# A third pair of k-tiles with seven block products in each gate and up chunk, and in the last down pass

## The chip, the cores and the metric

The kernel runs on one core of a Trainium2 chip. The metric is the device time in microseconds (us) of one execution; the median of several runs is what is compared. TensorE (PE in the views) multiplies, VectorE (DVE) and ScalarE (ACT) work element by element, SyncE (SP) issues the DMAs, GpSimd (POOL) is nearly idle here.

## The reference, cut to what matters

One transformer-like layer on 256 rows of 2048 channels, in float32: a SwiGLU feed-forward, a mixer (sparse attention beside a spatial gate), and a second SwiGLU feed-forward. The change touches the two feed-forwards only.

```python
D_MODEL, SEQ, D_FF = 2048, 256, 5632

def swiglu(h, w_gate, w_up, w_down):
    return (jax.nn.silu(h @ w_gate) * (h @ w_up)) @ w_down

x = x + 0.5 * swiglu(rms_norm(x, norm_ffn1), ffn1_w_gate, ffn1_w_up, ffn1_w_down)
...
x = x + 0.5 * swiglu(rms_norm(x, norm_ffn2), ffn2_w_gate, ffn2_w_up, ffn2_w_down)
```

## The kernel before

Every float32 product is made of three matmuls: weights and activations are each split into a high part that TensorE takes whole and a low rest (`split_to`, lines 228 and 229: a copy on ScalarE gives `wh`, a subtraction on VectorE gives `wl`), and high by high, low by high and high by low are added in PSUM. The three matmuls of a product are lines 322 to 324 in `gemm_seven` and 280 to 282 in the plain `gemm`; each has 512 columns.

A feed-forward (`ffn`) walks over 11 chunks of 512 hidden channels. A chunk multiplies the 256 rows by 512 gate columns and 512 up columns over 16 k-tiles of 128. The first chunk or chunks (two in the first feed-forward, one in the second, `plain`) use the plain `gemm`; in the second plain chunk of the first feed-forward the activations are rescaled as well (`rescale`), and the sums of activation blocks are made there (`x_sums`). The other 19 chunks of the two feed-forwards use `gemm_seven`. After 6 chunks, and again after the last 5, the hidden activations are multiplied by the down weights in two passes of 1024 output columns each (`half` 0 and 1), again with `gemm_seven`, over 12 and then 10 pairs of k-tiles.

`gemm_seven` takes the k-tiles in pairs. A pair with two tiles of rows and two blocks of 512 columns is a 2 by 2 by 2 product of blocks. An ordinary pair makes eight block products (24 matmuls) from two split tiles of 1024 columns. A pair in `seven` makes seven (21 matmuls), with Winograd's sums: four sums of weight blocks, which VectorE forms in lines 336, 337, 338 and 345, and four sums of activation blocks, formed once by `block_sums` (lines 500 to 503). Such a pair splits two tiles of 1024 columns of `w`, one of 1024 columns of `T` and one of 512 columns of `T`. The results P1, P5, P6 and P7 stay in banks of their own; once the last seven-product pair is done they are added to `e` (or to `xres`) by the stages of `early` (lines 603 to 613 for a chunk), one stage at each `tick()`, and ordinary pairs alone tick. P2 and P3 sit in the two `tr` banks, so matmuls into them show as `tr<-`.

At the end of a chunk VectorE reads P2, P3, P4 and C22 with lines 621 and 624, ScalarE makes the silu (line 622), VectorE the product (line 625). In the ticks of the next chunk the result is turned: ScalarE makes planes (line 377), a DMA transpose from SP's queue (line 379) turns them, ScalarE joins them (line 381), then they are split, and for up to four chunks of a part `sum_chunk` makes the activation sums of the down pass.

Raw weights have three buffers `w` of two k-tiles (1 MB each, loaded by two DMAs of 512 KB from SP's queue, line 566, or one of 1 MB, line 370); the split tiles have four buffers `wh` and four `wl`, `T` has two. The order of instructions on each engine is made by a scheduler ahead of time, so that it differs from the order in the source; each engine then works through its own list strictly in that order.

Of the kernel before, what the change touches and what calls it, by code (L numbers as in the profile page):

```python
# [13 lines left out]
F32 = mybir.dt.float32  # L14
# [7 lines left out]
P = 128  # L22
# [44 lines left out]
def block_kernel(ctx: ExitStack, tc: tile.TileContext, x, positions, norm_ffn1, ffn1_w_gate, ffn1_w_up,  # L67
                 ffn1_w_down, norm_mix, w_in, q_norm, k_norm, idx_k_norm, sgu_v_norm, sgu_w_s, sgu_b_s,
                 w_up_attn, w_up_sgu, w_out, norm_ffn2, ffn2_w_gate, ffn2_w_up, ffn2_w_down, out):
    nc = tc.nc  # L70
# [12 lines left out]
    def uid(s):  # L83
        cnt[0] += 1
        return f"{s}_{cnt[0]}"
# [7 lines left out]
    def bank(shape=None):  # L93
        return psA.tile(shape or [P, 512], F32, tag="acc", name=uid("acc"))

    def trbank(shape):
        return psT.tile(shape, F32, tag="tr", name=uid("tr"))
# [7 lines left out]
    def tick(n=1):  # L105
        for _ in range(min(n, len(pending))):
            pending.popleft()()
# [119 lines left out]
    def split_to(hi, lo, src):  # L227
        nc.scalar.copy(hi, src)  # L228
        nc.vector.tensor_sub(lo, src, hi.bitcast(F32))  # L229
# [59 lines left out]
    def split_wide(src):  # L289
        n = src.shape[-1]  # L290
        whi = wsp.tile([P, 1024], F32R, tag="wh", name=uid("wh"))
        wlo = wsp.tile([P, 1024], F32R, tag="wl", name=uid("wl"))
        split_to(whi[:, :n], wlo[:, :n], src)
        return [(whi[:, o:o + 512], wlo[:, o:o + 512]) for o in range(0, n, 512)]

    def gemm_seven(new_T, xs, sums, nk, load, seven, early):

        acc = {}
        total = {}
        np_ = nk // 2
        for name in ("P1", "P5", "P6", "P7"):
            total[name] = len(seven)
        for name in ("P2", "P3", "P4"):  # L310
            total[name] = len(seven) + 2 * (np_ - len(seven))
        total["C22"] = 2 * (np_ - len(seven))
        done = {k: 0 for k in total}

        def product(name, st, w):
            (sh, sl), (wh, wl) = st, w
            if name not in acc:
                acc[name] = trbank([P, 512]) if name in ("P2", "P3") else bank()
            first = done[name] == 0
            done[name] += 1  # L320
            last = done[name] == total[name]
            nc.tensor.matmul(acc[name], sh, wh, start=first, stop=False)  # L322
            nc.tensor.matmul(acc[name], sl, wh, start=False, stop=False)  # L323
            nc.tensor.matmul(acc[name], sh, wl, start=False, stop=last)  # L324

        left = len(seven)
        wait = None
        for g in range(np_):
            w = wraw.tile([P, 2048], F32, tag="w", name=uid("w"))
            load(2 * g, 2, w.rearrange("p (k c) -> p k c", k=2))  # L330
            if g in seven:
                A11, A12, A22 = xs(2 * g, 0), xs(2 * g + 1, 0), xs(2 * g + 1, 1)
                S1, S2, S3, S4 = sums(g)
                T = new_T()
                B11, B12, B21, B22 = (w[:, i * 512:(i + 1) * 512] for i in range(4))
                nc.vector.tensor_sub(T[:, 0:512], B12, B11)
                nc.vector.tensor_sub(B12, B22, B12)
                nc.vector.tensor_add(T[:, 512:1024], B12, B11)
                b11, t3 = split_wide(w[:, 0:1024])
                product("P1", A11, b11)  # L340
                product("P7", S3, t3)
                t1, t2 = split_wide(T[:, 0:1024])
                product("P5", S1, t1)
                product("P6", S2, t2)
                nc.vector.tensor_sub(T[:, 1024:1536], B21, T[:, 512:1024])
                b21, b22 = split_wide(w[:, 1024:2048])
                product("P2", A12, b21)
                product("P3", S4, b22)
                t4, = split_wide(T[:, 1024:1536])
                product("P4", A22, t4)  # L350
                left -= 1
                if left == 0:
                    wait = 2
            else:
                for kk in range(2):
                    k = 2 * g + kk
                    B = split_wide(w[:, kk * 1024:(kk + 1) * 1024])
                    for t, names in enumerate((("P2", "P3"), ("P4", "C22"))):
                        for j, name in enumerate(names):
                            product(name, xs(k, t), B[j])  # L360
                    if wait is not None:
                        wait -= 1
                        if wait == 0:
                            pending.extendleft(reversed(early(acc["P1"], acc["P5"], acc["P6"], acc["P7"])))
                    tick()
        return [[acc["P2"], acc["P3"]], [acc["P4"], acc["C22"]]]
# [136 lines left out]
        nc.vector.tensor_sub(s_[:, 3, :], A12, s_[:, 1, :])  # L503
        split_to(hi, lo, s_)

    XSEVEN = (0, 3)
    PARTS = ((0, 6, (4, 4)), (6, 5, (4, 2)))
    KP = 24

    def ffn(nrm, wg, wu, wd, after_chunk, first=0, lead=None, plain=1):  # L510
        with tc.tile_pool(name=uid("ffn"), bufs=1) as pool:
            def new_T():
                return pool.tile([P, 3 * 512], F32, tag="T", bufs=2, name=uid("T"))


            xSh = pool.tile([P, len(XSEVEN), 4, P], F32R, name=uid("xSh"))
            xSl = pool.tile([P, len(XSEVEN), 4, P], F32R, name=uid("xSl"))

            def x_sums(i, f=None):
                k = 2 * XSEVEN[i]  # L520
                if f is None:
                    f = ttile([P, 2, S])
                    nc.vector.tensor_add(f, nrm.h[:, k:k + 2, :].bitcast(F32), nrm.l[:, k:k + 2, :].bitcast(F32))
                block_sums(xSh[:, i], xSl[:, i], f[:, 0, 0:P], f[:, 1, 0:P], f[:, 0, P:S], f[:, 1, P:S])
# [4 lines left out]
            def xsums(g):  # L529
                i = XSEVEN.index(g)  # L530
                return [(xSh[:, i, c, :], xSl[:, i, c, :]) for c in range(4)]

            def rescale(kp):
                f = nrm.apply(kp)
                if kp in XSEVEN:
                    x_sums(XSEVEN.index(kp), f)

# [3 lines left out]

            for f0, nf, nseven in PARTS:
                last_part = f0 + nf == FF // 512
# [17 lines left out]
                for fi in range(nf):  # L561
# [32 lines left out]
                    else:  # L594
# [3 lines left out]
                        def early(P1, P5, P6, P7, e=e):  # L598
# [17 lines left out]
                            return [one, two, three, four]  # L616

                        b = gemm_seven(new_T, xx, xsums, KD, load, XSEVEN, early)
                        for t in range(NT):
                            sg = ttile()  # L620
# [15 lines left out]
                for half in range(2):  # L636
                    c0 = half * 1024

                    def early(P1, P5, P6, P7, c0=c0):
# [23 lines left out]
                        def five():  # L663
                            nc.vector.tensor_add(right, right, q["5"][:, None, :].to_broadcast([P, 2, 512]))

                        return [one, two, three, four, five]

                    b = gemm_seven(new_T, xs, sums, nf * 4, loader(wd[f0 * 512:(f0 + nf) * 512, :], c0, 1024),
                                   [2 * i for i in range(nseven[half])], early)
                    for t in range(NT):  # L670
# [396 lines left out]
```

## Time and profile before

| | |
|---|---|
| Median of 3 runs | 2054.71 us (2052.78 to 2056.4) |
| The profiled execution's own time | 2055.26 us |
| Its span, first to last instruction | 2053.5 us |
| PE busy | 2039.0 us (99%), 9124 matmuls |
| Weight loads (PEld) busy | 1695.1 us (83%) |
| DVE busy | 1574.2 us (77%) |
| ACT busy | 1230.7 us (60%) |

The own time is 1.8 us longer than the span: what lies before the first and after the last instruction. Busy time is the union of an engine's instructions; an average over the span mixes stages, so the stages are looked at one by one below.

### The profile page before, as it was taken

Reading aid. Unit: us, or ns where it says so; the run is one execution under the profiler, and the core shown is the slowest. Engines: PE = TensorE matmul, PEld = TensorE weight load, DVE = VectorE, ACT = ScalarE, POOL = GpSimd, SP = SyncE. Lnnn points to the kernel's source line nnn. Section 1 sums busy time; section 2 is a strip of 40 time slices with the busy share of each in tenths; the row PEclk is TensorE's granted clock in tenths of the full one; section 3 lists DMA queues with packets and bytes.
Section 4 is the critical chain, followed back from the end, with each engine's and each line's share of the span. In section 5 each row is a group of like instructions: output and inputs, shape, how many; then the busy total and the mean of one; then the engine's idle time right before and its main releaser. Section 6 shows DMA issues by size and latency. Waiting matters only on the chain.

```text
span 2053.5 us, 25205 instructions
## 1 busy us (share of the span) xinstructions
PE 2039.0 (99%) x9124; PEld 1695.1 (83%) x9124; DVE 1574.2 (77%) x2043; ACT 1230.7 (60%) x1482; POOL 33.8 (2%) x62
## 2 busy tenths in 40 slices
PE   8999999999999999999999999999999999999999
PEld 7888888888888898888888888888888888888887
DVE  6888888788889667877544467568888888788895
ACT  6666664465666566656544445576666644666663
POOL 1000000000000000110000000000000000000000
PEclk9999999999999999999999999999999999999999
DMA  7666665667666676586655567776677666676674
GB/s 257 187 213 211 226 202 204 205 201 229 195 200 220 201 243 210 178 232 186 205 193 201 186 195 229 215 220 195 202 219 222 196 212 206 200 224 207 195 232 148
DMA packets 251533, 426.13 MB, mean 208 GB/s; under 512 B 106664, under 2 KB 108768, under 8 KB 251408
## 3 DMA queue, kind: packets, MB, share of 16 engines
q1 hardware_dynamic: 250880, 423.29, 65.3%
q0 software_dynamic: 528, 1.23, 0.4%
q8 instruction: 71, 1.16, 0.2%
q14 instruction: 54, 0.44, 0.1%
HBM read 398.26 MB, written 2.10 MB: 195 GB/s over the span
## 4 chain that ended last, share of the span: by engine, by line
PE 51%; DMA 1%; ACT 1%; DVE 0%; issue 0%; SPq 0%; DVEq 0%; ACTq 0%
PE acc L282 7%; PE acc L281 7%; PE acc L280 7%; PE acc L324 6%; PE acc L322 6%; PE acc L323 6%; PE tr L322 5%; PE tr L324 5%; PE tr L323 5%; DMA tu<-pl 1%; DMA w<-in_ffn_w_up 0%; ACT wh L228 0%; DVE wl L229 0%; PE tr L959 0%; DVE xres L673 0%
## 5 line engine op out<-in xcount | busy, mean ns | idle before, releaser
L228 ACT CAST wh<-w 128x1024 fp32r<-128x1024 f32 (+2 forms) x768 | 785.5, 1035 | 595.9 <-PE acc L323 313.0
L229 DVE TENSOR_TENSOR wl<-w,wh 128x1024 fp32r<-128x1024 f32 (+2 forms) x768 | 914.1, 1199 | 256.6 <-ACT wh L228 249.8
L280 PE MATMUL acc<-wh,xTh 128*128 128x512 f32 (+1 forms) x864 | 333.3, 387 | 0.7 <-ACT wh L228 0.7
L281 PE MATMUL acc<-wh,xTl 128*128 128x512 f32 (+1 forms) x864 | 331.6, 384 | 0.0
L282 PE MATMUL acc<-wl,xTh 128*128 128x512 f32 (+1 forms) x864 | 313.9, 383 | 0.1
L322 PE MATMUL acc<-wh,xTh 128*128 128x512 f32 x532 | 207.0, 389 | 0.0
L323 PE MATMUL acc<-wh,xTl 128*128 128x512 f32 x532 | 207.0, 389 | 0.0
L322 PE MATMUL tr<-wh,xTh 128*128 128x512 f32 x494 | 192.3, 389 | 1.0 <-ACT wh L228 1.0
L323 PE MATMUL tr<-wh,xTl 128*128 128x512 f32 x494 | 192.2, 389 | 0.0
L324 PE MATMUL acc<-wl,xTh 128*128 128x512 f32 x532 | 191.0, 389 | 0.0
L280 PEld LDWEIGHTS acc<-wh,xTh 128*128 128x128 f32 x864 | 162.8, 188 | 30.8 <-ACT wh L228 1.3
L281 PEld LDWEIGHTS acc<-wh,xTl 128*128 128x128 f32 x864 | 162.8, 188 | 29.5
L282 PEld LDWEIGHTS acc<-wl,xTh 128*128 128x128 f32 x864 | 161.2, 188 | 30.2 <-DVE wl L229 0.5
L324 PE MATMUL tr<-wl,xTh 128*128 128x512 f32 x494 | 169.9, 389 | 0.0
L229 DVE TENSOR_TENSOR wl<-T,wh 128x1024 fp32r<-128x1024 f32 (+1 forms) x132 | 125.6, 952 | 43.9 <-ACT wh L228 33.6
L228 ACT CAST wh<-T 128x1024 fp32r<-128x1024 f32 (+1 forms) x132 | 110.3, 836 | 76.7 <-PE acc L323 64.8
L324 PEld LDWEIGHTS acc<-wl,xTh 128*128 128x128 f32 x532 | 99.9, 188 | 21.2 <-DVE wl L229 0.5
L323 PEld LDWEIGHTS acc<-wh,xTl 128*128 128x128 f32 x532 | 99.9, 188 | 20.8
L322 PEld LDWEIGHTS acc<-wh,xTh 128*128 128x128 f32 x532 | 99.8, 188 | 20.6
L323 PE MATMUL acc<-wh,hTl 128*128 128x512 f32 x296 | 115.2, 389 | 0.0
L322 PE MATMUL acc<-wh,hTh 128*128 128x512 f32 x296 | 115.1, 389 | 0.0
L322 PEld LDWEIGHTS tr<-wh,xTh 128*128 128x128 f32 x494 | 92.7, 188 | 20.5 <-ACT wh L228 1.3
(278 smaller groups left out, 2947.5 us busy)
## 6 DMA issues: line engine op xcount, KB each, us to landing
w<-in_ffn_w_down SPq DMA_DIRECT2D x88, 1024.0 KB, 5.0
w<-in_ffn_w_gate SPq DMA_DIRECT2D x175, 512.0 KB, 3.9
w<-in_ffn_w_up SPq DMA_DIRECT2D x175, 512.0 KB, 4.7
w<-in_w_in SPq DMA_DIRECT2D x72, 1024.0 KB, 5.0
w<-in_w_out SPq DMA_DIRECT2D x16, 1024.0 KB, 5.3
w<-in_w_in SPq DMA_DIRECT2D x16, 552.0 KB, 4.0
w<-in_w_up_attn SPq DMA_DIRECT2D x8, 1024.0 KB, 5.0
w<-in_w_up_sgu SPq DMA_DIRECT2D x8, 1024.0 KB, 5.1
```

What stands on the lines that cost most here:

```text
L228: nc.scalar.copy(hi, src)
L229: nc.vector.tensor_sub(lo, src, hi.bitcast(F32))
L280: nc.tensor.matmul(o_, sh, whj, start=(k == 0), stop=False)
L281: nc.tensor.matmul(o_, sl, whj, start=False, stop=False)
L282: nc.tensor.matmul(o_, sh, wlj, start=False, stop=(k == nk - 1))
L322: nc.tensor.matmul(acc[name], sh, wh, start=first, stop=False)
L323: nc.tensor.matmul(acc[name], sl, wh, start=False, stop=False)
L324: nc.tensor.matmul(acc[name], sh, wl, start=False, stop=last)
```

## The change

The weight sum for P4 (line 345) is no longer written to a third block of `T` ahead of the split of the lower k-tile, but over that k-tile's own block `B21`, after it has been split and its two products have been issued. `T` shrinks from three blocks to two. In every chunk of `gemm_seven` the pairs with seven products are 0, 2 and 4 of eight in place of 0 and 3, which takes a third set of activation sums in `xSh` and `xSl` and a third `x_sums` in each feed-forward. In the second down pass of the last part (ten pairs) they are 0, 2 and 4 in place of 0 and 2; the other down passes keep their four.

```diff
                 t1, t2 = split_wide(T[:, 0:1024])
                 product("P5", S1, t1)
                 product("P6", S2, t2)
-                nc.vector.tensor_sub(T[:, 1024:1536], B21, T[:, 512:1024])
                 b21, b22 = split_wide(w[:, 1024:2048])
                 product("P2", A12, b21)
                 product("P3", S4, b22)
-                t4, = split_wide(T[:, 1024:1536])
+                nc.vector.tensor_sub(B21, B21, T[:, 512:1024])
+                t4, = split_wide(B21)
                 product("P4", A22, t4)
...
-    XSEVEN = (0, 3)
-    PARTS = ((0, 6, (4, 4)), (6, 5, (4, 2)))
+    XSEVEN = (0, 2, 4)
+    PARTS = ((0, 6, (4, 4)), (6, 5, (4, 3)))
...
             def new_T():
-                return pool.tile([P, 3 * 512], F32, tag="T", bufs=2, name=uid("T"))
+                return pool.tile([P, 2 * 512], F32, tag="T", bufs=2, name=uid("T"))
```

## Rows read from the trace of the kernel before

**Rows 1.** The page, part 1 (busy time by engine) and PE's clock by slices.
```profile
PE 2039.0 (99%) x9124; PEld 1695.1 (83%) x9124; DVE 1574.2 (77%) x2043; ACT 1230.7 (60%) x1482; POOL 33.8 (2%) x62
...
PEclk9999999999999999999999999999999999999999
```

**Rows 2.** Busy time by stretch: two plain chunks, a chunk, three down passes.
```profile
core 0: us, PE busy (x) PEld busy (x) DVE busy (x) ACT busy (x) POOL busy (x), PEclk, DMA share, GB/s
54.00:100.00 46.00, 46.00 (x204) 37.53 (x203) 41.09 (x65) 30.00 (x36) 0.00 (x0) 1.00 0.63 192
184.50:226.66 42.16, 42.16 (x187) 34.91 (x186) 35.89 (x44) 27.50 (x32) 0.00 (x0) 1.00 0.68 212
605.92:656.48 50.56, 50.56 (x225) 41.87 (x224) 48.43 (x59) 33.87 (x38) 0.00 (x0) 1.00 0.65 218
656.48:710.24 53.76, 53.76 (x239) 44.52 (x238) 40.54 (x51) 35.90 (x51) 0.00 (x0) 1.00 0.64 199
1352.00:1396.70 44.70, 44.70 (x199) 37.02 (x198) 31.69 (x50) 33.76 (x53) 1.61 (x1) 1.00 0.68 194
1993.63:2046.59 52.96, 52.96 (x235) 43.87 (x234) 33.66 (x37) 22.20 (x24) 0.00 (x0) 1.00 0.46 159
```

**Rows 3.** DVE in order of time (start us, duration us): steps, no waits.
```profile
148.82 1.22 DVE L229 TENSOR_TENSOR wl<-w,wh 128x1024 fp32r<-128x1024 f32 x1
149.95 0.68 DVE L336 TENSOR_TENSOR T<-w 128x512 f32<-128x512 f32 x1
150.56 1.22 DVE L229 TENSOR_TENSOR wl<-w,wh 128x1024 fp32r<-128x1024 f32 x1
```

**Rows 4.** DVE's waits of one chunk in order of time, in brackets.
```profile
196.78 0.69 DVE L229 TENSOR_TENSOR hTl<-t,hTh 128x512 fp32r<-128x512 f32 x1 [0.51 <-ACT hTh L228]
...
201.12 0.29 DVE L500 TENSOR_TENSOR t<-t 128x128 f32<-128x128 f32 x1 [0.77 <-ACT t L381]
...
202.02 1.23 DVE L229 TENSOR_TENSOR wl<-w,wh 128x1024 fp32r<-128x1024 f32 x1 [0.42 <-ACT wh L228]
...
215.28 1.22 DVE L229 TENSOR_TENSOR wl<-w,wh 128x1024 fp32r<-128x1024 f32 x1 [0.68 <-ACT wh L228]
217.52 0.69 DVE L336 TENSOR_TENSOR T<-w 128x512 f32<-128x512 f32 x1 [1.01 <-DMA w<-in_ffn_w_up]
...
224.17 1.23 DVE L229 TENSOR_TENSOR wl<-T,wh 128x1024 fp32r<-128x1024 f32 x1 [1.49 <-ACT wh L228]
226.66 0.69 DVE L621 TENSOR_TENSOR t<-tr,e 128x512 f32<-128x512 f32 x1 [1.27 <-PE tr L324]
227.27 1.22 DVE L229 TENSOR_TENSOR wl<-w,wh 128x1024 fp32r<-128x1024 f32 x1
...
230.20 0.68 DVE L229 TENSOR_TENSOR wl<-T,wh 128x512 fp32r<-128x512 f32 x1
```

**Rows 5.** The page, part 6: weight loads, KB each, median us from issue to landing.
```profile
w<-in_ffn_w_gate SPq DMA_DIRECT2D x175, 512.0 KB, 3.9
w<-in_ffn_w_up SPq DMA_DIRECT2D x175, 512.0 KB, 4.7
```

**Rows 6.** All engines in order of time around PE's longest stop in a feed-forward.
```profile
1409.80 1.35 ACT L381 COPY t<-tu 128x1024 uint16<-128x1024 uint16 x1 [2.10 <-DMA tu<-pl]
...
1414.56 0.39 PE L323 MATMUL acc<-wh,xTl 128*128 128x512 f32 x1
...
1414.99 0.50 PE L324 MATMUL acc<-wl,xTh 128*128 128x512 f32 x1
...
1416.46 0.50 PE L322 MATMUL tr<-wh,xTh 128*128 128x512 f32 x1 [0.97 <-ACT wh L228]
...
1416.80 0.39 PE L323 MATMUL tr<-wh,xTl 128*128 128x512 f32 x1
```

**Rows 7.** Who waited for whom over the span: us in total, times, longest.
```profile
ACT wh L228 <- PE acc L323: 377.7, 288, 2.4
...
ACT t L381 <- DMA tu<-pl: 35.2, 40, 2.7
```

## The prediction

> **What bounds the kernel now.** The page comes first: PE is busy for 99% of the span at the full clock, DVE 77%, ACT 60% [rows 1]. A busy share alone does not say that PE sets the pace, so the second view is busy time by stretch [rows 2]. The chunk from 184.50 to 226.66 lies between two first readings of P2 (line 621) and lasts 42.16 us. It has two pairs with seven products and six with eight: 2 x 7 + 6 x 8 = 62 products, 186 matmuls, and 186 weight loads are counted. 42.16 / 186 = 0.2267 us a matmul, without a gap. The down pass from 656.48 has 2 x 7 + 8 x 8 = 78 products, 234 matmuls, at the same step 53.0 us; the window ends later, at another reading of the last results. So in the feed-forwards time is the number of matmuls times 0.2267 us, as long as VectorE and ScalarE deliver.
>
> How near are they to not delivering? In the same chunk DVE is busy 35.89 of 42.16 us, ACT 27.50 [rows 2]. The third view is DVE in order of time with its waits [rows 4]: 0.51, 0.77, 0.42, 0.68, 1.01, 1.49 and 1.27 us, 6.15 together. The last ones are the larger, and end on work that follows PE: ACT's cast of the next tile waits for PE to give back a `wh` buffer (377.7 us in all over the span [rows 7]), and line 621 waits for PE's last P2. DVE has run ahead there until it had nothing to do. The first three, 1.70 us, are of another kind: ACT is late with something.
>
> **The matmuls removed.** Each of the 19 seven-product chunks (9 in the first feed-forward, 10 in the second) turns one more pair, one product or three matmuls: 57. The second down pass of the last part turns one more pair in each feed-forward: 6. 63 x 0.2267 = 14.28 us. The step is taken from the whole chunk, so it has the weight load beside each matmul in it. The Trainium skill ("TensorE: Matmul & The Clock Gate", section "Wait — 56ns, not 53.3ns?") gives 215.7 ns between warm matmuls of 512 columns; by it the term would be 13.59 us, and the trace, at 226.7 ns in this kernel, does not agree and decides.
>
> **The work added.** A pair that turns gives DVE four sums of 512 columns, one split of 1024 and one of 512, and gives ACT the two casts. From start to start a 512-wide operation takes 0.60 us (149.95 to 150.56 shows 0.61), a 1024-wide one 1.13 [rows 3]: 4 x 0.605 + 1.13 + 0.60 = 4.15 us on DVE. By durations (0.68 and 1.22) it would be 4.62, the upper bound; the steps are right where instructions follow each other, since they overlap. ACT gets some 1.7 us (casts somewhat shorter than DVE's subtractions): 29.2 of a chunk, with room. The chunk after: 183 matmuls, 41.48 us of PE, and 40.04 us of DVE (40.51 by durations), 96.5%. The rest is 1.44 us in place of 6.27. This is the whole question.
>
> **Does PE still run without gaps at that load?** The trace before holds a near copy: the first down pass of the last part, 605.92 to 656.48 [rows 2]. It follows a chunk, has the same readings, silu, product and turning of that chunk in its first pairs, and seven-product pairs at 0, 2, 4 and 6, just the alternation that the chunk gets. DVE is busy 48.43 of 50.56 us, 95.8%, and PE 50.56 of 50.56. What differs is that a chunk must win back its lead each time. An ordinary pair costs PE 24 x 0.2267 = 5.44 us and DVE 2 x 1.13 = 2.26; a seven-product pair 4.76 and 6.41. In pairs 5 to 7 PE needs 16.3 us. DVE has 6.8 for their splits, 2.34 for the `early` stages (two of 0.60, one of 1.13) and 4.1 for what it prepares of the next pair 0 (three sums, two splits): 13.2. The lead is won back with 3 us over. At the start DVE is behind by some 3.6 us of readings and products plus 1.65 for each of pairs 0, 2 and 4, and gains 3.2 at pairs 1 and 3, less 1.2 and about 1.4 for the turned halves and `sum_chunk`: 5.25 after pair 0, 4.9 after pair 2, 4.7 after pair 4. The highest point is the one that the kernel before passes already without a gap.
>
> **The moved sum.** It now stands behind the split of `B21`, so 0.60 us that DVE did ahead of the boundary falls behind it, in the busiest stretch; ACT's cast of it and P4 follow. The write over `B21` needs that ACT has read it, which the low split before it has waited for already; no new wait. The raw buffer is given back after the split of the sum, not of `B21`: in [rows 4] these end at 230.88 and 228.49, so the load three pairs on is issued 2.4 us later, and behind it in SP's queue stand the next transposes and loads. A load lands 4.7 us after issue [rows 5], and two other pairs stand between, at least 2 x 2.26 us of DVE even if both are ordinary and some 10 us at PE's pace: hidden, I cost it at 0. If the cover goes, DVE's 1.01 us wait for a load at the end of the chunk grows by up to 2.4 us.
>
> **Smaller things.** The third `x_sums`: four operations of 0.29 us [rows 4] and a split of 0.60, 1.8 us at most, plus an addition of 0.60 in the second feed-forward. Their plain chunks have DVE at 41.09 of 46.0 and 31.69 of 44.7 us [rows 2]: hidden, 0. The two last down passes go from 40.54 and 33.66 us of DVE to 44.7 and 37.8, in about 53: 0. `early` starts one pair later, with five ticks left for four stages: 0. `T` and the activation sums trade the same space.
>
> **What a stop costs.** One row shows it: ACT, in order, waits 2.10 us for a late transpose, its casts come late, and PE stops [rows 6]. Steps of 0.43, 1.47 and 0.34 us in place of 0.2267 are 1.56 us lost. ACT waits for transposes 40 times [rows 7], and this one reached PE in force. With less lead more of them may. Bound below: this stop vanishes too, since the order is made anew, 1.56 us of gain; above: see the rivals. I take one more stop of 1.56 us, nearest to what the near copy shows.
>
> **Sum.** 14.28 - 1.56 = 12.7 us. The profiled 2055.26 us (span 2053.5) would become 2042.5; that execution is 0.55 above the median of 2054.71, so 2042.0 for the median.
>
> **Rivals.**
> (B) VectorE sets the pace in chunks. If the 1.70 us of waits for ACT stay as they are [rows 4], a chunk takes 40.04 + 1.70 = 41.74 us and not 41.48; the chunks give 19 x 0.42 = 8.0, the down passes 1.36, and the median is 2045.3. By durations, 42.21 us, the chunks give nothing and it is 2053 to 2054. For it: 1.44 us of room. Against it: 95.8% in the near copy without a gap, where DVE's waits shrank to 2.1 us.
> (C) Transposes reach PE. If five to nine of the 38 turned halves of these chunks each stop PE for 1.56 us, 7.8 to 14 us are lost and the time is 2048 to 2054.5: no difference. For it: the stop of [rows 6], in the second seven-product pair of a chunk. Against it: one in 40.
> (D) Slower: DVE's idle time is not lead but fixed, and VectorE is already the bound. The 6.27 us of a chunk would stay, 40.04 + 6.27 = 46.3 in place of 42.16; 19 x 4.15 = 79 us, 2134. It decides from 2.1 us of fixed idle time per chunk (42.16 - 40.04). For it: DVE's busy share is the highest next to PE's. Against it: PE's step has no gap, and DVE's longest waits end on PE. The Trainium skill ("Perfetto Trace Analysis", section "Identifying the Most-Contended Engine") judges TensorE by its weight loads, not by its matmul share, and VectorE by occupancy; here that is 34.91 against 35.89 of 42.16 us, so VectorE would be the engine to relieve, and at constant occupancy a chunk would take 47.0 us, 2147 in all; the gapless step speaks against it.
>
> **Chances.** The forecast, within 2038.8 to 2044: 0.60. B below 2050.6: 0.22. C, with the far end of B: 0.11. D, or stops past twelve: 0.07. 0.2% is 4.1 us, about what a measurement of this kernel can tell from no change; so faster (below 2050.6) 0.82, same 0.11, slower 0.07. Range: from 2038.8 (14.28 + 1.56 off the median) to 2050.0, leaving out 0.18.
>
> **What would show it.** Right: chunks 41.48 us apart between first readings by line 621, 9061 matmuls, DVE about 40 us busy in each, and its waits near the end of a chunk gone or small. Wrong: PE waiting for `wh` or `wl` after pairs 2 or 4 (B), such waits behind ACT's line 381 (C), chunks longer than 42.16 us with DVE at the same 85% (D); lines that wait for a load in the middle of a chunk would refute the cost of nothing for the late buffer. The prediction fails if the lead is not won back in pairs 5 to 7.

## The result, and the profile after

The changed kernel takes 2144.52 us (2141.86 to 2147.11), the one before 2054.55 in the same session: a ratio of 1.0439, 95% interval 1.0426 to 1.0452. The forecast was 2042. The profiled execution took 2142.05 us, its span is 2140.3.

The page's first part, as [rows 1] before:

```profile
PE 2070.3 (97%) x9061; PEld 1680.3 (79%) x9061; DVE 1668.7 (78%) x2180; ACT 1249.8 (58%) x1526; POOL 31.9 (1%) x62
```

The 63 matmuls are gone (9124 to 9061). DVE did 94.5 us more work, yet its share rose by one point only, because the span grew by 86.8 us as well.

Busy time by stretch, as [rows 2]: a chunk from one first reading by line 621 to the next, and the first down pass of the last part.

```profile
core 0: us, PE busy (x) PEld busy (x) DVE busy (x) ACT busy (x) POOL busy (x), PEclk, DMA share, GB/s
1839.89:1885.91 46.02, 43.71 (x188) 34.55 (x187) 39.65 (x51) 28.51 (x33) 0.00 (x0) 1.00 0.62 195
644.85:698.67 53.82, 52.94 (x231) 42.84 (x230) 48.87 (x58) 33.85 (x39) 0.00 (x0) 1.00 0.62 206
```

A chunk takes 46.02 us, not 41.48. (DVE's readings shift a little against PE, so that this one holds 187 weight loads; over all fifteen distances without a down pass between them the mean is 46.1 us for 183 matmuls.) DVE's work is what was forecast, 39.65 us, but its idle time has not shrunk: 6.37 us against 6.27. The down pass keeps its four seven-product pairs, and still its 230 matmuls, counted by weight loads, take 53.82 us where the old step gives 52.14. That points at something that slows a seven-product pair itself, and not only the third one of a chunk.

Who waited, over the span, as [rows 7] (us in all, times, longest). First ACT, then SP, then PE, and last the lines of ACT and SP in the kernel before:

```profile
ACT wh L228 <- DVE w L348: 84.1, 40, 5.7
...
ACT t L381 <- DMA tu<-pl: 63.0, 24, 4.4
```
```profile
SPq L566 <- DVE wl L229: 600.8, 143, 14.4
```
```profile
PE acc L322 <- ACT wh L228: 40.5, 43, 2.9
PE tr L322 <- ACT wh L228: 9.9, 46, 0.2
```
```profile
ACT wh L228 <- DVE T L345: 0.3, 1, 0.3
...
SPq L566 <- DVE wl L229: 456.3, 114, 7.6
```

Line 348 is the sum over `B21`. ACT waits for it 84 us; for the same sum in its old place (line 345) it had waited 0.3 us. The waits for transposes are fewer and three times as long: 63.0 / 24 = 2.6 us against 35.2 / 40 = 0.9 in [rows 7]. The longest wait of a load in SP's queue for DVE to free a raw buffer was 7.6 us before and is 14.4. PE now stops for ACT 43 times at matmuls into `acc` and 46 times, for at most 0.2 us, at those into `tr`.

One stop in order of time, in the chunk that begins at 1839.89 (start us, duration us, in brackets the wait before). DVE:

```profile
1839.89 0.68 DVE L621 TENSOR_TENSOR t<-tr,e 128x512 f32<-128x512 f32 x1
1840.49 1.22 DVE L229 TENSOR_TENSOR wl<-w,wh 128x1024 fp32r<-128x1024 f32 x1
...
1844.02 0.68 DVE L348 TENSOR_TENSOR w<-w,T 128x512 f32<-128x512 f32 x1
1844.62 1.41 DVE L625 SCALAR_TENSOR_TENSOR t<-t,rstd,t 128x512 f32<-128x512 f32 x2
1845.94 4.09 DVE L229 TENSOR_TENSOR wl<-w,wh 128x512 fp32r<-128x512 f32 x4
...
1856.57 0.69 DVE L336 TENSOR_TENSOR T<-w 128x512 f32<-128x512 f32 x1 [3.27 <-DMA w<-in_ffn_w_up]
```

SP's queue, all that it issued from 1833.7 to 1851:

```profile
1833.72 0.46 SPq L566 DMA_DIRECT2D w<-in_ffn_w_up  x1
1846.65 0.37 SPq L566 DMA_DIRECT2D w<-in_ffn_w_gate  x1
1847.07 0.46 SPq L566 DMA_DIRECT2D w<-in_ffn_w_up  x1
1848.92 0.37 SPq L566 DMA_DIRECT2D w<-in_ffn_w_gate  x1
1849.35 1.29 SPq L379 DMA_TRANSPOSE tu<-pl  x1
1850.68 0.57 SPq L566 DMA_DIRECT2D w<-in_ffn_w_up  x1
```

ACT and PE (from the view of all engines):

```profile
1855.31 1.35 ACT L381 COPY t<-tu 128x1024 uint16<-128x1024 uint16 x1 [4.19 <-DMA tu<-pl]
...
1856.09 0.39 PE L324 MATMUL tr<-wl,xSh 128*128 128x512 f32 x1
...
1857.47 1.56 ACT L228 CAST wh<-w 128x512 fp32r<-128x512 f32 x2
...
1858.13 0.50 PE L322 MATMUL acc<-wh,xTh 128*128 128x512 f32 x1 [1.66 <-ACT wh L228]
```

Pair 0's block is split by 1841.71, but its fourth sum starts at 1844.02 behind the readings of the last chunk, ACT's cast and DVE's products come between, and the split of the sum (the first, 512-wide, of the four from 1845.94) ends at 1846.6. At 1846.65 the next load starts; for 12.9 us SP had issued nothing. Then the loads for two pairs start within 4.0 us of each other, with the transpose among them. The transpose, issued at 1849.35, releases ACT 5.96 us later; ACT's casts stand behind line 381 in its list, and PE stops from 1856.5 to 1858.1. At the same time DVE waits 3.27 us for pair 4's load at line 336, which its order had put ahead of the split that pair 2 still needed.

This stop of the queue is no single case. From one issue to the next SP lets more than 10 us pass 25 times in the changed kernel, 24 of them in the feed-forwards, 12.2 to 15.0 us each, about one in every chunk and down pass. In the kernel before it does so twice, in the feed-forwards once, for 10.1 us, apart from the end of the program. And transposes land later. The view of the DMA issues (median us from issue to landing), before and after:

```profile
tu<-pl SPq DMA_TRANSPOSE x94, 3.0
```
```profile
tu<-pl SPq DMA_TRANSPOSE x94, 3.5
```

Of the 94, the 44 that turn hidden activations for ACT's line 381 have a median of 2.78 us before and 4.29 after. They do not stand behind the loads in SP's queue: before and after, SP issues them at most 1.7 us, mostly 0.03 us, after ACT has made the planes (the one above 0.13 us after). What is longer is the time from their issue to their landing, among the loads that have been let go together.

### The profile page after: what moved, and what is told of

It is laid out like the page before. It is cut to its first block, busy times and chain, and to the rows that moved or that the text cites. A ratio compares the mean times of both kernels' runs of the same rounds, so it can differ in the third digit from the quotient of the medians.

```text
span 2140.3 us, 25222 instructions
## 1 busy us (share of the span) xinstructions
PE 2070.3 (97%) x9061; PEld 1680.3 (79%) x9061; DVE 1668.7 (78%) x2180; ACT 1249.8 (58%) x1526; POOL 31.9 (1%) x62
## 4 chain that ended last, share of the span: by engine, by line
PE 74%; DMA 10%; ACT 7%; DVE 6%; issue 3%; SPq 0%; ACTq 0%; DVEq 0%
PE acc L280 11%; PE acc L281 11%; PE acc L282 11%; PE acc L324 7%; PE acc L322 7%; PE acc L323 7%; PE tr L322 6%; PE tr L323 6%; PE tr L324 6%; DMA tu<-pl 5%; ACT wh L228 4%; DMA w<-in_ffn_w_up 4%; DVE wl L229 2%; DMA w<-in_ffn_w_down 1%; ACT t L381 1%
## 5 line engine op out<-in xcount | busy, mean ns | idle before, releaser
L228 ACT CAST wh<-w 128x1024 fp32r<-128x1024 f32 (+2 forms) x855 | 819.4, 990 | 607.1 <-PE acc L281 228.0
L229 DVE TENSOR_TENSOR wl<-w,wh 128x1024 fp32r<-128x1024 f32 (+2 forms) x855 | 961.8, 1146 | 257.5 <-ACT wh L228 248.6
L323 PE MATMUL acc<-wh,xTl 128*128 128x512 f32 x494 | 194.6, 394 | 0.0
L322 PE MATMUL tr<-wh,xTh 128*128 128x512 f32 x437 | 175.2, 401 | 8.0 <-ACT wh L228 8.0
L323 PE MATMUL tr<-wh,xTl 128*128 128x512 f32 x437 | 171.2, 392 | 0.0
L324 PE MATMUL acc<-wl,xTh 128*128 128x512 f32 x494 | 168.7, 393 | 0.0
L324 PE MATMUL tr<-wl,xTh 128*128 128x512 f32 x437 | 147.9, 397 | 6.1 <-DVE wl L229 6.1
L229 DVE TENSOR_TENSOR wl<-T,wh 128x1024 fp32r<-128x1024 f32 x87 | 106.0, 1219 | 11.6 <-ACT wh L228 11.3
L322 PEld LDWEIGHTS tr<-wh,xTh 128*128 128x128 f32 x437 | 82.3, 188 | 41.0 <-ACT wh L228 24.6
L336 DVE TENSOR_TENSOR T<-w 128x512 f32<-128x512 f32 x87 | 59.9, 689 | 64.8 <-DMA w<-in_ffn_w_up 45.4
```

## The experiments

Two theories at first. **H, the hold:** a sum over `B21` keeps the raw buffer until the sum has been split; loads come late and in bunches, transposes queue behind them, ACT and DVE are held up in their fixed order. **L, the load:** at 96% VectorE cannot deliver (the rivals B and D). The changed place alone and the third pair alone tell them apart. Times are medians, ratios to the kernel before with their 95% interval.

**1. In place, two pairs.** The kernel before with the in-place sum and T of two blocks:

```diff
-                nc.vector.tensor_sub(T[:, 1024:1536], B21, T[:, 512:1024])
                 b21, b22 = split_wide(w[:, 1024:2048])
...
-                t4, = split_wide(T[:, 1024:1536])
+                nc.vector.tensor_sub(B21, B21, T[:, 512:1024])
+                t4, = split_wide(B21)
```

> The fourth weight sum in place over its raw block, T of two blocks, but the pairs as before (0 and 3; 4 and 2 in the last passes). Theory H (hold): the raw buffer is kept until the sum is split, so the load three pairs on, and the transposes behind it in SP's queue, come late and bunched; the changed kernel lost about 98 us more on PE than the one before over 87 seven-product pairs, 1.1 us a pair, so 66 pairs should lose some 40 to 75 us: 2095 to 2130. Theory L (load): VectorE has too much to do in a chunk with three pairs; the work here is that of before, so 2050 to 2060.

2100.53 us, 1.0227 (1.0212 to 1.0243). The pairs are those of before, VectorE's work too, and 47 us are lost. H is right about where; L has no part in this.

**2. Three pairs, the sum in T's first block.** The changed kernel, with

```diff
+                nc.vector.tensor_sub(T[:, 0:512], B21, T[:, 512:1024])
                 b21, b22 = split_wide(w[:, 1024:2048])
...
-                nc.vector.tensor_sub(B21, B21, T[:, 512:1024])
-                t4, = split_wide(B21)
+                t4, = split_wide(T[:, 0:512])
```

> The changed kernel, but the fourth sum goes into T's first block, ahead of the split of B21 and B22, so that the raw buffer is free when these are split. Same matmuls, same VectorE work (40 us a chunk). H: the gain that was forecast comes, 2040 to 2056. L: it stays slow, 2110 to 2145.

2067.53 us, 1.0069 (1.0054 to 1.0084): 77 us of the loss are gone, but 26 us remain above the forecast. Neither theory had this number.

**3. Control: the same with two pairs.** As 2, with the pairs of before.

> Control: the kernel before with the fourth sum in T's first block in place of a third one; pairs as before. Both theories: 2050 to 2060, no difference over 0.3 percent. If it is slower, writing the sum over the first block of T costs by itself, and the other run in T has to be read against it.

2053.67 us, 0.9999 (0.9990 to 1.0009). With two pairs, the sum in T's first block costs nothing.

**4. The last pass alone.**

```diff
-    PARTS = ((0, 6, (4, 4)), (6, 5, (4, 2)))
+    PARTS = ((0, 6, (4, 4)), (6, 5, (4, 3)))
```

> The kernel before with three pairs in the second pass of the last part (4 and 3) and nothing else. Two pairs more, six matmuls: 1.36 us. Both theories: 2050 to 2056; the passes from line 673 to line 673 should be 0.68 us shorter each. L would have it only if VectorE, at 44.7 of 53 us there, were already short.

2053.01 us, 0.9998 (0.9989 to 1.0007): below what can be told apart, and no harm.

**5. The hold without the place.** Experiment 3 with a small operation that keeps the raw block in use:

```diff
                 product("P4", A22, t4)
+                nc.vector.tensor_tensor(B21[:, 0:8], B22[:, 0:8], t4[1][:, 0:8].bitcast(F32), op=ALU.subtract)
```

> Two pairs a chunk and the sum in T, the version that took as long as before (2053.7), plus one subtraction of 8 columns on VectorE after the split of the fourth sum, which reads the upper and writes the lower end of the raw block: the sum is not in place, but the raw buffer is held as long as if it were. The 66 added instructions are some 0.1 us each, 4 to 7 us of VectorE in all. H: what costs is the hold, so most of the 47 us of the in-place run come back, 2085 to 2105. Rival (what costs is that the sum is made late, behind the split of its block, so that ScalarE waits for it): no hold effect, 2054 to 2062.

2087.76 us, 1.0163 (1.0148 to 1.0178). Of the 47 us of experiment 1, 34 come back with nothing but the hold. (The operation itself took 0.16 us, 66 times: some 10 us of DVE in all.)

**6. Extra work for VectorE.** Experiment 3 with, at an ordinary pair,

```diff
+                if spare is not None and g == 2:
+                    for i in range(7):
+                        nc.vector.tensor_sub(spare[:, 0:512], spare[:, 0:512], spare[:, 512:1024])
```

> Two pairs a chunk, sum in T, plus seven 512-wide subtractions on a scratch tile in every seven-product chunk, ahead of pair 2: 4.2 us of VectorE a chunk as a third pair brings, without its matmuls saved, its casts or its buffers. L: VectorE's load by itself stops PE; the run with three pairs and the sum in T lies 27 us above its sum of 2040.4, 1.4 us a chunk, so 2067 to 2082. Rival (the third pair costs by what it asks of loads, split buffers and order): 2054 to 2058.

2083.50 us, 1.0143 (1.0128 to 1.0158), which looks like L. It is not a test of it. The trace shows where the work went (the view of the tile, its first line the instruction with duration ns and first and last start, its last line the busy tenths in 40 slices):

```profile
L357 DVE TENSOR_TENSOR spare<-spare x133: 674/681/693, 2.0 to 1542.1; 128x512 f32<-128x512 f32 x133
...
busy tenths in 40 slices 3220000000000000000000000022210000000000
```

Operations that depend on nothing were moved by the scheduler to the front of each feed-forward. In the first, 43 of 63 start ahead of the first seven-product chunk and 20 in it; in the second, 21 of 70 start ahead and the other 49 in the first three seven-product chunks. The chunks after 160 us and after 1560 us had none, so the run does not say what 4.2 us a chunk cost. It does say what too much costs. One chunk of the second feed-forward with 18 of the operations, and the next one but one, with none:

```profile
1455.09:1501.95 46.86, 43.04 (x185) 34.01 (x184) 45.53 (x62) 27.65 (x31) 0.00 (x0) 1.00 0.60 191
...
1547.77:1589.93 42.16, 42.16 (x187) 34.91 (x186) 36.71 (x46) 27.82 (x32) 0.00 (x0) 1.00 0.66 213
```

With 18 more operations, 11.55 us of busy time by themselves, DVE is busy for 45.53 of 46.86 us, and PE stops; without them the chunk takes 42.16 us as before. Nearly all of the loss of some 30 us lies in the stretches with these operations. So VectorE's load can stop PE, at more than twice what a third pair brings. Experiment 12 fell to the same.

**7. Pairs 1, 3 and 5.** Experiment 2 with

```diff
-    XSEVEN = (0, 2, 4)
+    XSEVEN = (1, 3, 5)
...
-                    wait = 2
+                    wait = 1
```

> Three pairs, sum in T, at 1, 3 and 5 in place of 0, 2 and 4; the early stages start one k-tile earlier after the last pair, so that all four still fit. The readings of the chunk before then fall on an ordinary pair. If the remaining 27 us are VectorE falling behind right after the boundary, 2043 to 2057; if they come from the whole load or from the tail, 2062 to 2080.

2066.43 us, 1.0060 (1.0045 to 1.0075): as with 0, 2 and 4. Which of these pairs they are is not the cause.

**8. Three pairs, T of three blocks, the sum early.** The kernel before with

```diff
-    tmp = ctx.enter_context(tc.tile_pool(name="tmp", bufs=8))
+    tmp = ctx.enter_context(tc.tile_pool(name="tmp", bufs=6))
...
-    XSEVEN = (0, 3)
-    PARTS = ((0, 6, (4, 4)), (6, 5, (4, 2)))
+    XSEVEN = (0, 2, 4)
+    PARTS = ((0, 6, (4, 4)), (6, 5, (4, 3)))
```

> Three pairs (0, 2, 4; 4 and 3), the fourth sum in a third block of T and ahead of the splits, as in the kernel before; to make room the temporaries have six buffers in place of eight. If the remaining 27 us come from the sum being made behind the first split of T (ScalarE waited 57 us for it in that run), 2041 to 2052; if from load, 2062 to 2075. If six temporaries bind, slower than that, and PE's or VectorE's waits will name them.

2041.41 us, 0.9940 (0.9923 to 0.9956): faster than both kernels, and within 0.6 us of the forecast for the change. Its page, a chunk and most of the first down pass of the last part by stretch, and SP's queue at the start of that chunk, whose line 621 starts at 1844.08:

```profile
PE 2026.1 (99%) x9061; PEld 1683.6 (83%) x9061; DVE 1658.4 (81%) x2180; ACT 1259.6 (62%) x1526; POOL 31.9 (2%) x62
```
```profile
1844.08:1885.63 41.55, 41.55 (x185) 34.42 (x184) 39.89 (x51) 29.22 (x34) 0.00 (x0) 1.00 0.66 216
599.78:650.00 50.22, 50.22 (x223) 41.58 (x222) 47.52 (x57) 33.33 (x38) 0.00 (x0) 1.00 0.65 219
```
```profile
1845.92 0.37 SPq L566 DMA_DIRECT2D w<-in_ffn_w_gate  x1
1846.33 0.47 SPq L566 DMA_DIRECT2D w<-in_ffn_w_up  x1
1851.98 1.23 SPq L379 DMA_TRANSPOSE tu<-pl  x1
1853.32 0.52 SPq L566 DMA_DIRECT2D w<-in_ffn_w_gate  x1
```

DVE is busy 39.89 of 41.55 us, 96%, and PE has no gap. L as a cause of the loss falls with this row. The first load of the chunk starts 1.84 us after line 621, in the changed kernel 6.76; the next one follows 7.4 us later, behind a transpose, in place of 2.3.

**9. Control: six temporaries in the kernel before.**

> Control: the kernel before with six temporaries in place of eight, nothing else. If the 12.7 us that the run with a third block of T gained come from the third pair alone, this takes 2052 to 2057; if six temporaries by themselves made a better order, it lies below 2050.

2054.17 us, 1.0003 (0.9993 to 1.0012). The gain of 8 is not the temporaries'.

**10. The sum behind the split of T.** Experiment 8 with one order added:

```diff
+                with tc.issue_after(last_low[0].ins):
+                    nc.vector.tensor_sub(T[:, 1024:1536], B21, T[:, 512:1024])
                 b21, b22 = split_wide(w[:, 1024:2048])
```

> Three pairs, T of three blocks, six temporaries (the version at 2041.4), with one order added: the fourth sum is issued behind the low split of T's first two blocks, as it must be where it overwrites one of them. Same work, raw buffer free as before. Theory W (the late sum): ScalarE meets the cast of the sum in its list before the sum is there, so 2058 to 2070, near the 2067.5 of the run with the sum in T. Rival (that run lost by something else, such as T's two buffers): 2041 to 2047.

2047.20 us, 0.9965 (0.9952 to 0.9978): 5.8 us, well short of the 26 of experiment 2. The raw buffer is not held here: one load in the whole run waits for the sum, for 1.6 us.

**11. The hold on experiment 8.** The added line of experiment 5.

> The version at 2041.4 with the raw buffer held until the fourth sum has been split, by one subtraction of 8 columns on VectorE that reads and writes the raw block; the sum itself is early, in T. The hold cost 34 us with 66 pairs and a sum behind T's split; H: it costs by itself, some 0.3 to 0.6 us a pair on 87 pairs, 2070 to 2095. Rival (hold only hurts with a late sum, since an early sum lets the buffer go earlier): 2043 to 2058.

2076.71 us, 1.0111 (1.0096 to 1.0126): 35.3 us for the hold alone, with an early sum. It hurts by itself.

**12. The extra work spread.** Experiment 6 with one operation at each ordinary pair, two at the last.

> The run with seven extra subtractions a chunk (2083.5), with them spread over the ordinary pairs, one each and two in the last, in place of seven in a row ahead of pair 2. If it is the row of seven in the busiest stretch that stopped PE, 2054 to 2063; if any 4.2 us more of VectorE cost it, 2070 to 2085.

2083.06 us, 1.0141 (1.0126 to 1.0156). The operations ended up in the same places; it tells no more than 6.

Experiments 8, 10 and 11 left about 60 us of the change without a name. Four more:

**13. The sum behind its own split.** As 10, ordered behind the split of `B21` and `B22`, into T's third block.

> Three pairs, T of three blocks, six temporaries, the fourth sum ordered behind the low split of B21 and B22, as late as in the change, but written to T's third block: the raw buffer goes free with the sum, not with its split. If lateness alone costs, more than the 5.8 us of the sum behind T's split: 2055 to 2080. If not: 2044 to 2052.

2064.64 us, 1.0051 (1.0036 to 1.0066): 23.2 us. This is not lateness alone. The sum still reads the raw block, so the buffer goes free only with it: 67 waits of loads end on the sum (350 us, longest 10.0), where in experiment 10 it was one. But the long stops of SP's queue are gone: over 10 us only twice, once at the end of the program.

**14. Late and held.** Experiment 13 with the added line of experiment 5.

> The same with the raw buffer held until the split of the sum, by a subtraction of 8 columns: lateness and hold as in the change, without writing in place. If these two are the whole cause, 2125 to 2155, near the 2144.5 of the change; if costs only add, near 2041.4 + 35 + what the run beside this one shows, 2080 to 2105, and something else of the change is still unnamed.

2133.14 us, 1.0391 (1.0376 to 1.0407): 91.7 us, far above 23.2 + 35.3 = 58.5. The two together cost nearly as much as the change's 103.

ACT's waits for the fourth sum (line 351) and SP's for the holding operation (line 354) in this kernel:

```profile
ACT wh L230 <- DVE T L351: 127.2, 58, 4.6
```
```profile
SPq L383 <- ACT wh L230: 366.4, 52, 17.0
SPq L570 <- DVE w L354: 295.0, 52, 13.3
```

Line 570 are the loads, line 383 the transposes. SP stands up to 13.3 us before a load until the hold ends, and up to 17.0 us before a transpose until ACT gets to its planes; the loads behind that transpose wait with it. So the way is not quite that of the change: SP's queue stops for more than 10 us 36 times here, and 21 of these stops end with a transpose, one of 25 in the changed kernel. What the runs with a hold share is the late landing of transposes, by the view of the DMA issues 2.8 us in experiments 8 and 13, which have no hold until the split, and 3.5 and 3.7 in 11 and 14.

**15. Experiment 2 with six temporaries.**

> The run with three pairs and the sum over T's first block (2067.5), with six temporaries. If its 20 us above the ordered sum (2047.2) came from the order that the scheduler made with eight, 2043 to 2052; if from writing over the first block, 2062 to 2070.

2066.15 us, 1.0062 (1.0047 to 1.0077), as with eight. What probably made 2 slower than 10 is in DVE's order in the trace of experiment 2:

```profile
1842.83 1.22 DVE L229 TENSOR_TENSOR wl<-T,wh 128x1024 fp32r<-128x1024 f32 x1
1843.96 1.22 DVE L229 TENSOR_TENSOR wl<-w,wh 128x1024 fp32r<-128x1024 f32 x1
1845.10 0.68 DVE L345 TENSOR_TENSOR T<-w,T 128x512 f32<-128x512 f32 x1
```

The sum, which has to wait for the split of the block that it overwrites, was put behind the split of `B21` too, as in experiment 13. As there, loads wait for it: 46 waits of SP end on the sum (183 us), and the time is nearly that of 13.

**16. The changed kernel with six temporaries.**

> The changed kernel with six temporaries. The control moved the kernel before by nothing (2054.2). If the loss of the change is its raw buffers, 2135 to 2150; if the accident of one order is a large part, it moves by 20 us or more either way.

2143.41 us, 1.0435 (1.0417 to 1.0453). The temporaries do not matter to the loss. Against the accident of one order it says less, since SP's queue stops at nearly the same places as in the changed kernel; experiments 1, 5, 11 and 14, in orders of their own, say more.

## Why the prediction was wrong

**What held.** The matmuls removed: 63, and PE's step. The work added: 40.04 us of DVE a chunk were forecast, 39.65 and 39.89 are measured. That PE runs without gaps at that load, argued from the near copy: experiment 8 shows a chunk of 41.55 us where 41.48 was forecast, and the whole gains 2054.16 - 2041.41 = 12.75 us where 12.7 was the sum. The agreement to a tenth is luck: the interval of that ratio spans 9 to 16 us, and the 1.56 us that were taken off for one more stop did not come, since PE's waits for ACT at line 322 are 0.3 us in experiment 8. The two profiled spans differ by 14.0 us, nearly the matmuls alone. The sum was right for the third pairs, and missed the other half of the change.

**The step that failed** is the moved sum: "hidden, I cost it at 0", and before it "no new wait". It has three faults, each with its price.

1. The delay. I took the raw buffer's release as 2.4 us later, from the ends of two splits of the old order [rows 4]. That was the distance between them when the sum was ready. Made late, the sum has to be formed, cast and split behind the readings of the last chunk: the first load of the chunk starts 6.76 us after line 621, and 1.84 in experiment 8, 4.9 us later.
2. The cover. I set one load's landing against the DVE time of two pairs, as if each load stood alone; the transposes and loads behind it were named and given no price. SP's queue stands for 12.9 us, then the loads go out together, and a transpose issued among them lands late: 4.29 us in the median against 2.78. That transpose, and not the held load itself, is what stops ACT and then PE in the stop shown. The price of the hold alone is 35.3 us (experiment 11), and 34 with two pairs (experiment 5).
3. The wait. The write over `B21` indeed waits for nothing new, but ACT's cast of the sum does: it had been ready, and now ACT meets it in its list before it is there, 84.1 us in 40 waits. The price of lateness alone is 5.8 us behind the split of T (experiment 10); behind the split of its own block it is 23.2, with a shorter hold in it (experiment 13).

Together lateness and hold cost 91.7 us (experiment 14), over half as much again as the two apart; why they do more than add was not measured. The change lies at 2144.5 - 2041.4 = 103 us; the last 11 were not separated. With two pairs the sum in place costs 47 us by itself (experiment 1), so it would have been slower without the third pair, too.

**The rivals.** D gave 2134 us, near the result, by idle time that stays; it did stay, 6.37 us. But its reason, VectorE as the bound, is refuted by experiment 8, where the idle time falls to 1.66 us at the same work. The Trainium skill's reading by occupancy ("Perfetto Trace Analysis", "Identifying the Most-Contended Engine") gave 2147 and is no better for being close: PE was the engine that set the pace in experiment 8, with its weight loads busy 34.42 us and DVE 39.89 of 41.55. C named transposes that reach PE. ACT waits 63.0 us for them in 24 waits, and in the stop shown one reaches PE, but as a consequence of the hold, which C did not have. B's 2045 to 2054 did not come. The Trainium skill ("Perfetto Trace Analysis", section "Optimization Strategy") says that the same gap repeating on the engine that should be saturated can mean that there is not enough space for the next tile to be allocated. The trace agrees: PE's waits for ACT repeat, 43 and 46 of them, 50.4 us, and the space that comes late is the raw buffer. I did not weigh it.

**What my own list would have shown.** It named lines that wait for a load in the middle of a chunk as the sign against a free late buffer: line 336 at 1856.57, 3.27 us. The signs that were meant to tell the rivals apart came as well and did not: a chunk longer than 42.16 us with DVE at 86% (D), PE waiting for `wh` at pair 2 (B), and that wait behind line 381 (C). Each follows from the late buffer too.

**What stays open.** The 11 us between experiment 14 and the change, and why lateness and hold together cost more than their sum. How much more than a third pair's 4 us a chunk VectorE would take: with 14 and with 18 more operations of 512 columns in a chunk PE stops (experiment 6: 45.82 and 46.86 us), and no run lies below that.

## What to carry to other kernels

An operation that is written over its own input keeps the input's buffer until the result is consumed; before calling that free, find the load that takes that buffer next, what stands behind it in the queue, and what will be in flight when the delayed loads go out together. Count the release from the last consumer in its new place, not from the distance in the old order, and price lateness and hold together. And measure the halves of an edit apart: here the arithmetic gained 12.7 us and the space that paid for it lost 103, while two temporaries less paid for it at no cost that could be measured.

## What was not expected of the hardware

The longest stop of the changed kernel's feed-forwards, but for their first 10 us, came in the first seven-product chunk. PE in order of time, and that stretch by window:

```profile
106.53 0.40 PE L324 MATMUL tr<-wl,xSh 128*128 128x512 f32 x1
109.87 0.80 PE L322 MATMUL acc<-wh,xTh 128*128 128x512 f32 x1 [2.94 <-ACT wh L228]
110.46 0.63 PE L323 MATMUL acc<-wh,xTl 128*128 128x512 f32 x1
110.89 0.63 PE L324 MATMUL acc<-wl,xTh 128*128 128x512 f32 x1
```
```profile
109.80:116.20 6.40, 6.33 (x15) 4.94 (x16) 4.61 (x5) 6.40 (x9) 0.00 (x0) 0.51 0.77 247
```

After 2.94 us without a matmul the steps are 0.43 us for 6 us, at a granted clock of 0.51, the lower level of 1.2 GHz, and then 0.227 again. Such stretches follow stops at 110, 205, 318, 731 and 1987 us, 39 steps in all, some 39 x 0.20 = 8 us of the loss. Not every stop is followed by one: the 1.66 us before 1858.13, shown above, are not. The kernel before and experiment 8 have no such stretch in their feed-forwards but for the first matmuls of all: up to 14 us steps of 0.43 us stand in all three kernels, there with the granted clock given as 1.00.
